# A ring tile of their own for the modulation units, and X's rows read back two per pair, in a one-core mLSTM, convolution and SwiGLU step

## The chip, the cores and the metric

The kernel runs on one core of a Trainium2 chip. The metric is the device time of one launch in microseconds; lower is better. The time before is the median of three runs: 1648.85 us, from 1646.58 to 1649.88.

## The reference

One layer of a diffusion backbone works on 640 tokens (128 of a context, 512 latent) of width 1024:

```python
mod = silu(cond) @ w_mod + b_mod                     # nine vectors of 1024 per condition
sh1, sc1, g1, shm, scm, gm, sh2, sc2, g2 = split(mod, 9)
h = rmsnorm(x, norm_g[0]) * (1 + sc1) + sh1
x = x + 0.5 * g1 * swiglu(h, ffn1_w1, ffn1_w2)       # (silu(a) * b) @ w2, inner width 2816
h = rmsnorm(x, norm_g[1]) * (1 + scm) + shm
z = h @ w_in + b_in                                  # q, k, v, o, gates, b, c, x, two merge gates
ml = (o * norm(mlstm_bidir(q, k, v, ...))) @ w_ml_out
sc = (bg * conv3(cg * xs)) @ w_sc_out
x = x + gm * ((sigmoid(gml) * ml + sigmoid(gsc) * sc) @ w_o)
h = rmsnorm(x, norm_g[2]) * (1 + sc2) + sh2
x = x + 0.5 * g2 * swiglu(h, ffn2_w1, ffn2_w2)       # then a final rmsnorm
```

All inputs are float32. There are two conditions (context and latent), so each of the nine modulation vectors is a product of two rows with a 1024 x 1024 piece of `w_mod`.

## The kernel before

The 640 tokens are two halves of 320. Activations lie transposed, 128 channels by 320 tokens. For float32 accuracy each operand is split into a high and a low part (ScalarE, ACT, copies the high part, line 75; VectorE, DVE, subtracts for the low one, line 79), and each product takes three matmuls on TensorE (PE; lines 288 to 290, in `three`).

**Elements.** The work is a list of elements. A plain element (`plain_el`) multiplies one block of a weight matrix, 128 columns by all rows, with both halves. A pair element (`pair_el`) does two blocks by two with seven products in place of eight; the sums of weights it needs are made by DVE (`ws`, line 270). The FFN runs in three groups of inner blocks (8, 8, 6), each with its w1 pairs and then its w2 blocks; the w2 blocks of the last group have 6 x 128 rows, 384 KB. PSUM tiles `ps` (four) take the products; DVE evacuates them, on line 360 in an FFN's w1 pairs, on 1020 and 2032 and 2072 in the products with w2, w_ml_out and w_sc_out.

**Weight loads.** `load_more` issues them on SyncE's queue (SP), in the order of one list `raws`, and each takes the next tile of a ring. A weight block and a modulation unit are both `[128, 1024]` float32 (512 KB) and share the ring `wr` with five tiles; a half tile `wq` serves the summed pairs. An instruction on SP waits until the ring's oldest tile has been read for the last time, and what is behind it in SP's queue waits as well. `cast_more` makes the casts up to four ahead of PE in the program, with six tiles each of `wh` and `wl`.

**Modulation units.** While other work runs, the vectors needed later are formed from `w_mod` in units of 512 KB. `mod_half` uses PE for them (line 649). `mod_dve` uses DVE: for each of two 128-row pieces and each condition a multiply and add with a column of silu(cond) (lines 767 and 769, accumulating into `ma`, `x` or `H` tiles). `with_own` and `with_units` hang units onto elements: the load goes behind the element's own loads in `raws`, and the reads are run as fillers among its products. In `with_units`, `places` says how many units each element gets; without it they are spread evenly.

**X.** The residual X (eight tiles, 128 x 640) is moved to DRAM while an FFN runs (`xd<-x`) and read back by `x_in` on GpSimd's queue (POOL) for the last group. `x_whole` reads all eight rows at one point of that group's third pair. The same function `more_of` serves both FFNs. Saved activation halves come back on the same queue (`HT3h`, `HT4h` and so on, line 1045).

Of the kernel before, what the change touches and what calls it, by code (L numbers as in the profile page):

```python
# [7 lines left out]
F32 = mybir.dt.float32  # L8
# [4 lines left out]
P = 128  # L13
D = 1024
KT = 8
# [29 lines left out]
def mixer_step(ctx: ExitStack, tc: tile.TileContext, x_prompt, x_sample, state_C, state_n, state_m,  # L45
# [33 lines left out]
            V.tensor_sub(lo, raw, f32(hi))  # L79


    RAWB, HALFB, OPB, SB, AHEAD = 5, 1, 6, 3, 4
    raws, ops = [], []
    rtile, optile, rdone = {}, {}, set()
    ptr = {"dma": 0, "sum": 0, "cast": 0, "use": 0, "held": 0, "hold": False, "cap": 1 << 20}
    fill = []
    turns, accs = {"wr": [], "wq": []}, []

    def drain(left=0):
        while len(fill) > left:  # L90
# [2 lines left out]
    def load_more(upto=1 << 20):  # L93
        while ptr["dma"] < min(upto, len(raws)):
            n = ptr["dma"]
            kind = getattr(raws[n], "kind", "wr")
            seq, bufs = turns[kind], RAWB if kind == "wr" else HALFB
            if len(seq) >= bufs and seq[-bufs] not in rdone:
                return
            seq.append(n)  # L100
            rtile[n] = ring.tile([P, 1024 if kind == "wr" else 512], F32, name=kind, bufs=bufs)
            raws[n](rtile[n])
            if hasattr(raws[n], "more"):
                accs.append((n, raws[n].more))
            ptr["dma"] += 1
# [89 lines left out]
    def element(raws_, ops_, emit):  # L195
        return {"raws": raws_, "ops": ops_, "emit": emit}
# [419 lines left out]
    PO = {}  # L616
# [92 lines left out]
    def with_own(pairs, ch, *last):  # L709

        us, fs = zip(*[mod_half(ch, half, True) for half in range(2)])
        out = []
        for p, el in enumerate(pairs):
            el = dict(el, raws=list(el["raws"]))
            fill = []
            if p < 4:
                units = us[p // 2][2 * (p % 2):2 * (p % 2) + 2]
                at_ = len(el["raws"])
                el["raws"] += [load for load, _ in units]

                def go(units=units, at_=at_, el=el):
                    tiles = [raw(el["base"] + at_ + i) for i in range(2)]
                    for i in range(2):
                        units[i][1](tiles[i])
                    rdone.update((el["base"] + at_, el["base"] + at_ + 1))
                    load_more()
                fill = [step(lambda: None), step(go), step(lambda: None)]
            if p == 2:
                fill[0] = step(fs[0][0])
                fill[2:] = [step(f) for f in fs[0][1:]]  # L730
            if p == 4:
                fill = [step(fs[1][0]), step(lambda: None)] + [step(f) for f in (*fs[1][1:], *last)]
            el["fill"] = fill
            out.append(el)
        return out

    def mod_mid(ch, half):
        us, fs = mod_half(ch, half)
        els = []
        for i, (load, emit) in enumerate(us):  # L740
            def go(w, emit=emit, last=(i == 3)):
                emit(w)
                if last:
                    soon.append(fs[0])
                    lazy.extend(fs[1:])
            els.append(dict(element([load], [], go), calm=True))
        return els

    def mod_dve(ch, halves, wide, joint=False):
# [54 lines left out]
    def with_units(main, units, spare=0, places=None):  # L804
# [3 lines left out]
        e = 0  # L808
        post = []
        due = [sum(places[:i + 1]) for i in range(len(main))] if places else None  # L810
        for i, el in enumerate(main):
# [4 lines left out]
            while e < m and (e < due[i] if places else e * n < (i + 1) * m):  # L816
                load, fns, more = units[e]
                at_ = len(el["raws"])
                el["raws"].append(load)
                for j, fn in enumerate(fns):  # L820
                    def go(fn=fn, at_=at_, el=el, last=(j == len(fns) - 1)):
                        fn(raw(el["base"] + at_))
# [383 lines left out]
    hd = {(o, k, i): hdr[8 * q + 2 * k + i] for q, o in enumerate(("T3", "T4")) for k in range(4) for i in range(2)}  # L1206
    PO["u_x"] = ExitStack()
    PO["un"] = 15

    def open_u():  # L1210
        PO["u"] = PO["u_x"].enter_context(pool("u"))
# [67 lines left out]
    def first_head(blocks):  # L1279
# [11 lines left out]
        def two(k0):  # L1291
# [1 line left out]
                for i, col0 in enumerate((0, DFF)):  # L1293
                    half_rows(ffn1_w1, col0, k0)(t[:, 512 * i:512 * i + 512])
            return load
        loads = [two(0), blocks[2][0]] + [u[0] for u in units[:RING]] + [two(4)] + [b[0] for b in blocks[3:]]
        part = lambda t, c: {"raws": [t], "n": 512, "src": lambda o: rtile[o["base"] + t][:, c:c + 512]}
        l2 = 2 + RING
        ops_ = [part(0, 0), part(0, 512), part(1, 0), part(1, 512), part(l2, 0), part(l2, 512)]
# [135 lines left out]
    def close_early():  # L1435
        early_x.close()
        st_x.close()
        PO["hq"] = ctx.enter_context(pool("hq", side="right"))

    uel = [step(lambda i=i: up[i][1](EARLY_T["up", i])) for i in range(4)]  # L1440
    qsc, qsh = [step(f) for f in UPQ[0][0]], [step(f) for f in UPQ[1][0]]
# [34 lines left out]
    prog += qsh[1:]  # L1476
    later = [lambda h=h, k=k: scale_x(h, k, RBS[h]) for h in (0, 1) for k in range(4, 8)]
    ptr["cap"] = 0
    def x_whole():
        for m in range(KT):  # L1480
            x_in(m)

    def x_end():
        while PO["x_end"]:
            PO["x_end"].pop(0)()

    def more_of(p):
        return {0: {p: {0: [lambda: h_away("T3", "T4")]}}, 1: {0: {4: [x_end]}},
                2: {0: {4: [x_end, lambda: PO.pop("xs")]}, 2: {1: [x_whole]}}}
    head, els = ffn(ffn1_w1, ffn1_w2, G1, after_lists(1, SHM), first_head, 3, (8, 8, 6), more_of(4),  # L1490
                    ({4, 5, 6, 7}, {4, 5, 6, 7}, ()), {0, 2}, {0: (2, 2, 1), 1: (2, 2, 1), 2: (3, 2)})
    PO["ma_x"] = ExitStack()
# [2 lines left out]
        gate_weights()  # L1495

    def open_ma():
        PO["ma"] = PO["ma_x"].enter_context(pool("ma"))

    def ma_wide():  # L1500
# [612 lines left out]
    conv = []  # L2113
    for m in range(0, KT, 2):
        if m:
            conv += [pair_el(*cx_pair(m), G), pair_el(*cx_pair(m + 1), G)]
        conv.append(pair_el(*bg_pair(m), G, spare_v=True))
    conv += weave([pair_el(*gsc_pair(m)) for m in range(0, KT, 2)], [step(lambda: None)] * 3 + [step(t_in(0))])
    prog += with_units(conv, mod_dve(SH2, (0,), m_wide), places=[1, 0, 0] * 3 + [1] + [0] * 4)
# [21 lines left out]
    def y_part(m, h):  # L2141
        def f():
# [4 lines left out]
            for i in range(3):  # L2147
                if h:
                    if m == 0:
                        YT[1, i] = ring.tile([P, 1024], F32, name="wr", bufs=RAWB)  # L2150
                    V.tensor_mul(YT[1, i][:, m * P:(m + 1) * P], p[:, i * P:(i + 1) * P],
                                 FN[q][:, (m % 2) * P:(m % 2 + 1) * P])
                    continue
# [95 lines left out]
```

## Time and profile before

| | |
|---|---|
| median of three runs | 1648.85 us |
| profiled execution | 1645.83 us, of which 1643.9 us is its span |
| PE, DVE, ACT, POOL busy | 99%, 80%, 54%, 20% of the span |
| DMA | 248.68 MB, mean 151 GB/s |
| clock granted to TensorE | 0.997 on average |
| largest wait of PE inside the program | 3.1 us, on DVE line 360 |

The profile comes from one execution. A group row ends with busy time and mean duration in ns; a row of waits gives the engine and line that waited, the engine and line that ended the wait, total, number and longest; a row of the timeline gives start, duration, engine, line, operation, `out<-in` and, in brackets, idle time of the engine just before and what ended it. Buffer numbers are left out of names there. In a row of windows the numbers after the window are the length and, for PE, PE's weight loads, DVE, ACT and POOL, the busy time; then the granted clock of TensorE (PEclk), DMA's share and GB/s.

### The profile page before, as it was taken

Reading aid. Unit: us, or ns where it says so; the run is one execution under the profiler, and the core shown is the slowest. Engines: PE = TensorE matmul, PEld = TensorE weight load, DVE = VectorE, ACT = ScalarE, POOL = GpSimd, SP = SyncE. Lnnn points to the kernel's source line nnn. Section 1 sums busy time; section 2 is a strip of 40 time slices with the busy share of each in tenths; the row PEclk is TensorE's granted clock in tenths of the full one; section 3 lists DMA queues with packets and bytes.
Section 4 is the critical chain, followed back from the end, with each engine's and each line's share of the span. In section 5 each row is a group of like instructions: output and inputs, shape, how many; then the busy total and the mean of one; then the engine's idle time right before and its main releaser. Section 6 shows DMA issues by size and latency. Waiting matters only on the chain.

```text
span 1643.9 us, 29669 instructions
## 1 busy us (share of the span) xinstructions
PE 1620.0 (99%) x10997; PEld 1573.2 (96%) x10997; DVE 1308.9 (80%) x2738; ACT 883.1 (54%) x1957; POOL 325.5 (20%) x457
## 2 busy tenths in 40 slices
PE   8999999999999999999999999999999999999998
PEld 5999999999989999999999999999999999999997
DVE  6878878978778878788897899879778877786765
ACT  5656555645466656555561455542276665565543
POOL 2132311130021322121121222001133113113002
PEclk9999999999999999999999999999999999999999
DMA  9698966793452434342367433457468768468522
GB/s 323 179 263 174 231 137 135 183 279 113 132 179 81 114 90 107 72 118 68 97 196 243 120 103 91 111 160 225 133 177 182 157 134 197 102 137 194 170 81 64
DMA packets 333200, 248.68 MB, mean 151 GB/s; under 512 B 11763, under 2 KB 306042, under 8 KB 333056
## 3 DMA queue, kind: packets, MB, share of 16 engines
q1 hardware_dynamic: 278256, 168.84, 35.8%
q0 software_dynamic: 54768, 77.95, 21.7%
q8 instruction: 86, 1.41, 0.4%
q14 instruction: 58, 0.48, 0.1%
q10 hardware_dynamic: 32, 0.01, 0.0%
HBM read 210.48 MB, written 36.28 MB: 150 GB/s over the span
## 4 chain that ended last, share of the span: by engine, by line
PE 84%; DVE 6%; DMA 3%; ACT 3%; issue 2%; SPq 1%; POOL 0%; ACTq 0%; DVEq 0%; POOLq 0%
PE ps L288 26%; PE ps L289 25%; PE ps L290 25%; DMA wr<-in_ffn_w_dram 3%; DVE wl L79 2%; PE ax L1793 2%; PE ax L1824 2%; PE ax L1796 1%; ACT wh L75 1%; PE ax L1770 1%; DVE ws L270 1%; ACT Uh L934 0%; SPq L627 0%; DVE Uh L926 0%; PE ax L778 0%
## 5 line engine op out<-in xcount | busy, mean ns | idle before, releaser
L79 DVE TENSOR_TENSOR wl<-wr,wh 128x512 fp32r<-128x512 f32 (+1 forms) x397 | 277.9, 709 | 86.2 <-ACT wh L75 84.1
L79 DVE TENSOR_TENSOR wl<-ws,wh 128x512 fp32r<-128x512 f32 x308 | 212.9, 691 | 62.9 <-ACT wh L75 62.5
L75 ACT CAST wh<-wr 128x512 fp32r<-128x512 f32 (+1 forms) x399 | 235.7, 606 | 36.8 <-DMA wr<-in_w_ml_out_dram 14.0
L75 ACT CAST wh<-ws 128x512 fp32r<-128x512 f32 x308 | 189.1, 620 | 97.9 <-DVE ws L270 83.2
L288 PE MATMUL ps<-HT4h,wh 128*128 128x320 f32 x440 | 139.5, 317 | 4.2 <-DVE t L360 4.0
L289 PE MATMUL ps<-HT4l,wh 128*128 128x320 f32 x440 | 137.1, 312 | 0.6 <-DVE HT4l L79 0.5
L288 PE MATMUL ps<-Uh,wh 128*128 128x320 f32 x440 | 137.3, 312 | 0.0
L290 PE MATMUL ps<-HT4h,wl 128*128 128x320 f32 x440 | 136.6, 310 | 0.0
L289 PE MATMUL ps<-Ul,wh 128*128 128x320 f32 x440 | 136.0, 309 | 0.0
L290 PE MATMUL ps<-Uh,wl 128*128 128x320 f32 x440 | 135.7, 308 | 0.0
L288 PE MATMUL ps<-HT3h,wh 128*128 128x320 f32 x388 | 122.0, 314 | 0.7 <-ACT ps L347 0.5
L288 PE MATMUL ps<-H11h,wh 128*128 128x320 f32 x376 | 119.6, 318 | 0.5 <-ACT H11h L75 0.5
L289 PE MATMUL ps<-HT3l,wh 128*128 128x320 f32 x388 | 119.9, 309 | 0.0
L290 PE MATMUL ps<-HT3h,wl 128*128 128x320 f32 x388 | 119.9, 309 | 0.0
L235 POOL DMA_DIRECT2D wr<-in_ffn_w_dram x48 | 62.3, 1448 | 282.6 <-DMA wr<-in_ffn_w_dram 115.9
L289 PE MATMUL ps<-H11l,wh 128*128 128x320 f32 x376 | 117.0, 311 | 0.7 <-DVE H11l L79 0.4
L288 PE MATMUL ps<-H21h,wh 128*128 128x320 f32 x376 | 117.5, 312 | 0.0
L290 PE MATMUL ps<-H11h,wl 128*128 128x320 f32 x376 | 116.6, 310 | 0.0
L290 PE MATMUL ps<-H21h,wl 128*128 128x320 f32 x376 | 116.3, 309 | 0.0
L289 PE MATMUL ps<-H21l,wh 128*128 128x320 f32 x376 | 116.0, 309 | 0.0
L288 PE MATMUL ps<-H22h,wh 128*128 128x320 f32 x344 | 107.9, 314 | 0.0
L289 PE MATMUL ps<-H22l,wh 128*128 128x320 f32 x344 | 106.5, 310 | 0.4
(489 smaller groups left out, 4943.7 us busy)
## 6 DMA issues: line engine op xcount, KB each, us to landing
wr<-in_ffn_w_dram SPq DMA_DIRECT2D x94, 512.0 KB, 5.7
wr<-in_w_in_dram SPq DMA_DIRECT2D x72, 512.0 KB, 3.9
wr<-in_w_mod_dram SPq DMA_DIRECT2D x59, 512.0 KB, 4.3
xd<-x POOLq DMA_DIRECT2D x56, 320.0 KB, 6.9
wr<-in_ffn_w_dram SPq DMA_DIRECT2D x52, 256.0 KB, 4.4
wr<-in_ffn_w_dram POOLq DMA_DIRECT2D x48, 256.0 KB, 5.4
x<-xd POOLq DMA_DIRECT2D x24, 320.0 KB, 8.0
early<-in_w_mod_dram SPq DMA_DIRECT2D x13, 512.0 KB, 8.9
```

The costliest lines, as they stand in the source:

```text
L75: A.copy(hi, raw)
L79: V.tensor_sub(lo, raw, f32(hi))
L235: queue.dma_start(t[:, 512 * o:512 * o + 512].rearrange("p (k n) -> p k n", k=4), dap(w, (row0 + 512 * half) * ncol + col0, [[ncol, P], [P ...
L270: engine.tensor_add(t, part(o, a), part(o, b))
L288: PE.matmul(ps, hi[:, ws], ah, start=start, stop=False, skip_group_check=True)
L289: PE.matmul(ps, hi[:, ws], al, start=False, stop=False, skip_group_check=True)
L290: PE.matmul(ps, lo[:, ws], ah, start=False, stop=stop, skip_group_check=True)
L1770: PE.matmul(p[:, :P], S["k", dt][:, sl], S["q", dt][:, sl], start=(dt == 0), stop=(dt == 1))
L1793: PE.matmul(p2[:, :DH + 1], S["q", dt][:, sl], S["C"][d][:, dt, :], start=(dt == 0), stop=(dt == 1))
L1796: PE.matmul(p1[:, :DH + 1], S["p", ch][:, d, :], PO["vt"][:, ch, :], start=True, stop=True)
L1824: PE.matmul(p[:, :DH + 1], kw[:, dt * P:(dt + 1) * P], PO["vt"][:, ch, :], start=True, stop=True)
```

## The change

There are two parts. First, units no longer share the five tiles of `wr`. `RAWB` gives `wr` four tiles, a new kind `wu` one, and a new kind `wv` one, which lives in a pool of its own from `close_early` to `open_ma` and serves the first FFN's first group alone. In `with_own` each two units take `wu` and `wv`. In `with_units` with `places` the first unit of an element takes `wu`, others `wr`; without, every other unit takes `wu`. `mod_mid` alternates, the third early unit of `first_head` takes `wu`, and so does one of three tiles of the last output. Second, `x_whole` is gone: the steps at index 1 and 4 of four pairs of the last group (2 to 5) each read one row of X. The line that builds `conv` is only written in another way.

```diff
@@ -79,12 +79,18 @@
             V.tensor_sub(lo, raw, f32(hi))
 
 
-    RAWB, HALFB, OPB, SB, AHEAD = 5, 1, 6, 3, 4
+    RAWB, OPB, SB, AHEAD = {"wr": 4, "wu": 1, "wv": 1, "wq": 1}, 6, 3, 4
     raws, ops = [], []
     rtile, optile, rdone = {}, {}, set()
     ptr = {"dma": 0, "sum": 0, "cast": 0, "use": 0, "held": 0, "hold": False, "cap": 1 << 20}
     fill = []
-    turns, accs = {"wr": [], "wq": []}, []
+    turns, accs = {k: [] for k in RAWB}, []
+
+    def of_kind(kind, load):
+        def f(t):
+            load(t)
+        f.kind = kind
+        return f
 
     def drain(left=0):
         while len(fill) > left:
@@ -94,11 +100,12 @@
         while ptr["dma"] < min(upto, len(raws)):
             n = ptr["dma"]
             kind = getattr(raws[n], "kind", "wr")
-            seq, bufs = turns[kind], RAWB if kind == "wr" else HALFB
+            seq, bufs = turns[kind], RAWB[kind]
             if len(seq) >= bufs and seq[-bufs] not in rdone:
                 return
             seq.append(n)
-            rtile[n] = ring.tile([P, 1024 if kind == "wr" else 512], F32, name=kind, bufs=bufs)
+            rtile[n] = (PO["wv"] if kind == "wv" else ring).tile([P, 512 if kind == "wq" else 1024], F32, name=kind,
+                                                                 bufs=bufs)
             raws[n](rtile[n])
             if hasattr(raws[n], "more"):
                 accs.append((n, raws[n].more))
@@ -716,7 +723,7 @@
             if p < 4:
                 units = us[p // 2][2 * (p % 2):2 * (p % 2) + 2]
                 at_ = len(el["raws"])
-                el["raws"] += [load for load, _ in units]
+                el["raws"] += [of_kind(kind, load) for kind, (load, _) in zip(("wu", "wv"), units)]
 
                 def go(units=units, at_=at_, el=el):
                     tiles = [raw(el["base"] + at_ + i) for i in range(2)]
@@ -743,7 +750,7 @@
                 if last:
                     soon.append(fs[0])
                     lazy.extend(fs[1:])
-            els.append(dict(element([load], [], go), calm=True))
+            els.append(dict(element([of_kind(("wu", "wr")[i % 2], load)], [], go), calm=True))
         return els
 
     def mod_dve(ch, halves, wide, joint=False):
@@ -816,7 +823,8 @@
             while e < m and (e < due[i] if places else e * n < (i + 1) * m):
                 load, fns, more = units[e]
                 at_ = len(el["raws"])
-                el["raws"].append(load)
+                other = any(getattr(q, "kind", "") == "wu" for q in el["raws"]) if places else e % 2
+                el["raws"].append(of_kind("wr" if other else "wu", load))
                 for j, fn in enumerate(fns):
                     def go(fn=fn, at_=at_, el=el, last=(j == len(fns) - 1)):
                         fn(raw(el["base"] + at_))
@@ -1206,6 +1214,7 @@
     hd = {(o, k, i): hdr[8 * q + 2 * k + i] for q, o in enumerate(("T3", "T4")) for k in range(4) for i in range(2)}
     PO["u_x"] = ExitStack()
     PO["un"] = 15
+    PO["wv_x"] = ExitStack()
 
     def open_u():
         PO["u"] = PO["u_x"].enter_context(pool("u"))
@@ -1293,7 +1302,7 @@
                 for i, col0 in enumerate((0, DFF)):
                     half_rows(ffn1_w1, col0, k0)(t[:, 512 * i:512 * i + 512])
             return load
-        loads = [two(0), blocks[2][0]] + [u[0] for u in units[:RING]] + [two(4)] + [b[0] for b in blocks[3:]]
+        loads = [two(0), blocks[2][0]] + [u[0] for u in units[:RING - 1]] + [of_kind("wu", units[RING - 1][0]), two(4)] + [b[0] for b in blocks[3:]]
         part = lambda t, c: {"raws": [t], "n": 512, "src": lambda o: rtile[o["base"] + t][:, c:c + 512]}
         l2 = 2 + RING
         ops_ = [part(0, 0), part(0, 512), part(1, 0), part(1, 512), part(l2, 0), part(l2, 512)]
@@ -1436,6 +1445,7 @@
         early_x.close()
         st_x.close()
         PO["hq"] = ctx.enter_context(pool("hq", side="right"))
+        PO["wv"] = PO["wv_x"].enter_context(pool("wv"))
 
     uel = [step(lambda i=i: up[i][1](EARLY_T["up", i])) for i in range(4)]
     qsc, qsh = [step(f) for f in UPQ[0][0]], [step(f) for f in UPQ[1][0]]
@@ -1476,17 +1486,14 @@
     prog += qsh[1:]
     later = [lambda h=h, k=k: scale_x(h, k, RBS[h]) for h in (0, 1) for k in range(4, 8)]
     ptr["cap"] = 0
-    def x_whole():
-        for m in range(KT):
-            x_in(m)
-
     def x_end():
         while PO["x_end"]:
             PO["x_end"].pop(0)()
 
     def more_of(p):
         return {0: {p: {0: [lambda: h_away("T3", "T4")]}}, 1: {0: {4: [x_end]}},
-                2: {0: {4: [x_end, lambda: PO.pop("xs")]}, 2: {1: [x_whole]}}}
+                2: {0: {4: [x_end, lambda: PO.pop("xs")]},
+                    **{2 + p: {i: [lambda m=2 * p + i // 3: x_in(m)] for i in (1, 4)} for p in range(4)}}}
     head, els = ffn(ffn1_w1, ffn1_w2, G1, after_lists(1, SHM), first_head, 3, (8, 8, 6), more_of(4),
                     ({4, 5, 6, 7}, {4, 5, 6, 7}, ()), {0, 2}, {0: (2, 2, 1), 1: (2, 2, 1), 2: (3, 2)})
     PO["ma_x"] = ExitStack()
@@ -1495,6 +1502,7 @@
         gate_weights()
 
     def open_ma():
+        PO["wv_x"].close()
         PO["ma"] = PO["ma_x"].enter_context(pool("ma"))
 
     def ma_wide():
@@ -2113,7 +2121,7 @@
     conv = []
     for m in range(0, KT, 2):
         if m:
-            conv += [pair_el(*cx_pair(m), G), pair_el(*cx_pair(m + 1), G)]
+            conv += [pair_el(*cx_pair(m + i), G) for i in range(2)]
         conv.append(pair_el(*bg_pair(m), G, spare_v=True))
     conv += weave([pair_el(*gsc_pair(m)) for m in range(0, KT, 2)], [step(lambda: None)] * 3 + [step(t_in(0))])
     prog += with_units(conv, mod_dve(SH2, (0,), m_wide), places=[1, 0, 0] * 3 + [1] + [0] * 4)
@@ -2147,7 +2155,8 @@
             for i in range(3):
                 if h:
                     if m == 0:
-                        YT[1, i] = ring.tile([P, 1024], F32, name="wr", bufs=RAWB)
+                        YT[1, i] = ring.tile([P, 1024], F32, name=("wu", "wr")[i > 0],
+                                             bufs=RAWB[("wu", "wr")[i > 0]])
                     V.tensor_mul(YT[1, i][:, m * P:(m + 1) * P], p[:, i * P:(i + 1) * P],
                                  FN[q][:, (m % 2) * P:(m % 2 + 1) * P])
                     continue
```

The order of the instructions on PE, SP and POOL is the same in both kernels; what differs on SP is the tile that a load takes and so what it waits for. Line numbers move by 7 to 9. Of SP's queue in the first FFN's last group, these are the rows around the w2 blocks before (`wr_5273`, `wr_5408` and `wr_5466` are units, the others blocks):

```order
L620 DMA wr_5273<-in_w_mod_dram 128x2x512
L218 DMA wr_5333<-in_ffn1_w2_dram 128x6x128
L620 DMA wr_5408<-in_w_mod_dram 128x2x512
L218 DMA wr_5428<-in_ffn1_w2_dram 128x6x128
L620 DMA wr_5466<-in_w_mod_dram 128x2x512
L218 DMA wr_5578<-in_ffn1_w2_dram 128x6x128
L218 DMA wr_5580<-in_ffn1_w2_dram 128x6x128
```

and now:

```order
L627 DMA wu_5329<-in_w_mod_dram 128x2x512
L225 DMA wr_5331<-in_ffn1_w2_dram 128x6x128
L627 DMA wu_5568<-in_w_mod_dram 128x2x512
L225 DMA wr_5570<-in_ffn1_w2_dram 128x6x128
L627 DMA wu_5628<-in_w_mod_dram 128x2x512
L225 DMA wr_5630<-in_ffn1_w2_dram 128x6x128
L225 DMA wr_5632<-in_ffn1_w2_dram 128x6x128
```

The units `wu_5329`, `wu_5568` and `wu_5628` follow each other in one tile, so each load waits for the last read of the unit before it; blocks `wr_5570` and `wr_5630`, formerly `wr_5428` and `wr_5578`, stand behind them as before.

On DVE at the same place (line 79 the low casts, 769 the reads of a unit, 1020 the evacuations), before:

```order
L79 TENSOR_TENSOR Ul_5535<-t3_5499,Uh_5534 128x320
L79 TENSOR_TENSOR wl_5541<-wr_5428,wh_5540 128x512
L79 TENSOR_TENSOR wl_5545<-wr_5428,wh_5544 128x256
L794 TENSOR_TENSOR modT_131<-ax_5525,bmT_129 128x4 x2
L769 SCALAR_TENSOR_TENSOR ma_5267<-wr_5273,cm_93,ma_5267 128x512 x2
L769 SCALAR_TENSOR_TENSOR ma_5310<-wr_5273,cm_93,ma_5310 128x512 x2
L1020 SCALAR_TENSOR_TENSOR x_4936<-ps_5538,modT_131,x_4936 128x128
L1020 SCALAR_TENSOR_TENSOR x_4936<-ps_5538,modT_131,x_4936 128x192
L1020 SCALAR_TENSOR_TENSOR x_4936<-ps_5539,modT_131,x_4936 128x320
L79 TENSOR_TENSOR wl_5603<-wr_5578,wh_5602 128x512
L79 TENSOR_TENSOR wl_5607<-wr_5578,wh_5606 128x256
L769 SCALAR_TENSOR_TENSOR ma_5267<-wr_5408,cm_93,ma_5267 128x512 x2
```

and now:

```order
L79 TENSOR_TENSOR Ul_5533<-t3_5497,Uh_5532 128x320
L801 TENSOR_TENSOR modT_131<-ax_5523,bmT_129 128x4 x2
L776 SCALAR_TENSOR_TENSOR ma_5263<-wu_5329,cm_93,ma_5263 128x512 x2
L776 SCALAR_TENSOR_TENSOR ma_5306<-wu_5329,cm_93,ma_5306 128x512 x2
L1028 SCALAR_TENSOR_TENSOR x_4938<-ps_5536,modT_131,x_4938 128x128
L1028 SCALAR_TENSOR_TENSOR x_4938<-ps_5536,modT_131,x_4938 128x192
L1028 SCALAR_TENSOR_TENSOR x_4938<-ps_5537,modT_131,x_4938 128x320
L79 TENSOR_TENSOR wl_5593<-wr_5570,wh_5592 128x512
L79 TENSOR_TENSOR wl_5597<-wr_5570,wh_5596 128x256
L776 SCALAR_TENSOR_TENSOR ma_5263<-wu_5568,cm_93,ma_5263 128x512 x2
L776 SCALAR_TENSOR_TENSOR ma_5306<-wu_5568,cm_93,ma_5306 128x512 x2
```

The two casts of the block behind unit 5408 (now 5568) have moved from ahead of the reads of unit 5273 (now 5329) to behind the evacuation after them, and those of the next block behind the reads of the next unit and its evacuation.

SP's queue in w_sc_out before, where units and blocks alternate in one ring:

```order
L620 DMA wr_13743<-in_w_mod_dram 128x2x512
L218 DMA wr_13771<-in_w_sc_out_dram 128x8x128
L620 DMA wr_13773<-in_w_mod_dram 128x2x512
L218 DMA wr_13857<-in_w_sc_out_dram 128x8x128
L620 DMA wr_13859<-in_w_mod_dram 128x2x512
L218 DMA wr_13945<-in_w_sc_out_dram 128x8x128
L620 DMA wr_13947<-in_w_mod_dram 128x2x512
L218 DMA wr_14031<-in_w_sc_out_dram 128x8x128
```

and now, where every other unit is `wu`:

```order
L627 DMA wr_13739<-in_w_mod_dram 128x2x512
L225 DMA wr_13767<-in_w_sc_out_dram 128x8x128
L627 DMA wu_13859<-in_w_mod_dram 128x2x512
L225 DMA wr_13861<-in_w_sc_out_dram 128x8x128
L627 DMA wr_13863<-in_w_mod_dram 128x2x512
L225 DMA wr_13949<-in_w_sc_out_dram 128x8x128
L627 DMA wu_14033<-in_w_mod_dram 128x2x512
L225 DMA wr_14035<-in_w_sc_out_dram 128x8x128
```

The blocks `wr_13767` to `wr_14035` stand where `wr_13771` to `wr_14031` did; `wr_13861` (formerly `wr_13857`) and `wr_14035` (formerly `wr_14031`) are now behind a unit that takes the tile of the unit two before it, and wait until that one has been read. On DVE and ACT the only other move is here, two casts that come after a unit's reads and an evacuation and not before them.

POOL's queue at the reads of X in the first FFN now, with what each waits for (DMASW counts earlier DMAs of this queue):

```order
L1041 DMA xd_133<-x_852 128x640 [waits DMASW2_49,DVE_49,Activation_49]
L1041 DMA xd_133<-x_853 128x640 [waits DMASW3_49,Activation_49]
L2093 DMA x_4938<-xd_133 128x640 [waits DMASW4_49]
L2093 DMA x_5006<-xd_133 128x640 [waits DMASW5_49]
L2093 DMA x_5097<-xd_133 128x640 [waits DMASW6_49]
L2093 DMA x_5165<-xd_133 128x640 [waits DMASW7_49]
L2093 DMA x_5265<-xd_133 128x640 [waits DMASW0_49]
L2093 DMA x_5333<-xd_133 128x640 [waits DMASW1_49]
L2093 DMA x_5422<-xd_133 128x640 [waits DMASW2_49]
L2093 DMA x_5478<-xd_133 128x640 [waits DMASW3_49]
```

Before, the same eight stand in the same place with the same waits; only the tiles' numbers, which count allocations, have spread out.

## The prediction

> **What bounds the kernel now.** I read the page first (busy times, then the chain), then the waits by engine, then the timeline and windows around every load that the change moves.
>
> ```profile
> PE 1620.0 (99%) x10997; PEld 1573.2 (96%) x10997; DVE 1308.9 (80%) x2738; ACT 883.1 (54%) x1957; POOL 325.5 (20%) x457
> PE ps L288 <- DVE t L360: 4.0, 3, 3.1
> PE ps L288 <- ACT ps L332: 0.6, 1, 0.6
> PE ps L288 <- ACT H11h L75: 0.5, 1, 0.5
> SPq L218 <- DVE ws L270: 527.0, 63, 20.2
> ```
>
> TensorE (PE) is busy for 99% of the span, so a change gains only what PE still waits for, and loses whatever makes PE wait. The largest wait inside the program is one of 3.1 us, behind line 360 on VectorE (DVE). SyncE's queue (SPq) does wait, 527 us in one group alone: it stands at the head of a ring that is full, which is how loads are issued many microseconds before their casts. This lead is what the change spends.
>
> The 3.1 us wait stands where X's rows come back in the first FFN:
>
> ```profile
> x<-xd POOLq DMA_DIRECT2D x8, 320.0 KB, 8.9
> wr<-in_ffn_w_dram SPq DMA_DIRECT2D x3, 512.0 KB, 12.3
> 344.77 0.37 SPq L620 DMA_DIRECT2D wr<-in_w_mod_dram  x1
> 350.31 5.12 SPq L218 DMA_DIRECT2D wr<-in_ffn_w_dram  x2
> 354.38 0.67 DVE ma L769
> 355.07 12.31 DMA wr<-in_ffn_w_dram
> 367.40 0.69 DVE L270 TENSOR_TENSOR ws<-wr 128x512 f32<-128x512 f32 x1 [4.15 <-DMA wr<-in_ffn_w_dram]
> 371.02 0.64 PE L288 MATMUL ps<-HT4h,wh 128*128 128x320 f32 x1 [3.11 <-DVE t L360]
> 370.00:372.00 2.00, 0.98 (x4) 0.98 (x5) 2.00 (x4) 0.62 (x1) 0.00 (x0) 0.50 0.00 0
> 372.00:376.80 4.80, 4.80 (x20) 4.80 (x20) 3.92 (x9) 2.31 (x5) 0.00 (x0) 0.50 0.39 113
> 376.80:380.00 3.20, 3.20 (x23) 3.20 (x23) 2.83 (x6) 1.76 (x4) 0.00 (x0) 1.00 0.55 164
> ```
>
> The first two rows are transfers issued from 342 to 370 us (number, size, median us to landing); then come two rows of SyncE's queue, a unit and two weight blocks, and two pieces of the chain. The weight load issued at 355.07, right after a unit's last read by DVE, shares the chip with eight transfers of X and takes 12.3 us. DVE stands still for 4.15 us, PE for 3.11. The windows (PEclk is the third number from the end) show the granted clock at 0.50 from PE's restart to 376.80: 5.8 us at half speed, 2.9 us lost. The whole place costs about 6.0 us, and it is the only sizeable prize.
>
> **The change part by part.** *X two rows per pair.* POOL's queue has the eight `x<-xd` in the same order, directly behind each other, in both kernels (rows in the section on the change), and nothing is put between them. In the program they wait for no engine, only for earlier DMAs, so writing them later in the program does not hold them back: they go out together as before. Cost and gain 0, in the second FFN too, whose PE has no such wait.
>
> *A ring of one for units.* A unit's load must now wait for the last read (L769) of the unit before it, and since SyncE issues in order, each weight block queued behind that unit waits too. I took every SP load's new releasers and put them on the times of this trace. Where the lead stays 7 us or more I count nothing: all of the mLSTM, the convolution and the second FFN. The early units (to about 165 us, ring tiles `wu` and `wv`) come earlier, up to 21 us; with PE's waits there being single ones of at most 0.6 us (rows above), that is worth −0.3 us, between −1.1 and 0. Four places are left.
>
> *(1) 344 to 372 us.* The unit issued at 344.8 goes out at 355.1 (behind the `DVE ma L769` above), and the two weight blocks at 355.6 and 356.0 instead of 350.3 and 355.1: all three inside X's burst. Against this, the burst ends earlier, since 0.5 MB of SP's loads are no longer mixed into its first half. If all is short the place is gone: −6.0. If the last block lands 4 us later: +4. The nearest row is the 12.3 us landing; with 0.9 us later issue I take +0.8.
>
> *(2) 416 to 450 us, the w2 blocks of the last group.*
>
> ```profile
> 415.99 0.37 SPq L620 DMA_DIRECT2D wr<-in_w_mod_dram  x1
> 418.76 0.37 SPq L218 DMA_DIRECT2D wr<-in_ffn_w_dram  x1
> 426.39 12.69 SPq L218 DMA_DIRECT2D wr<-in_ffn_w_dram  x5
> 429.69 2.98 DVE L769 SCALAR_TENSOR_TENSOR ma<-wr,cm,ma 128x512 f32<-128x512 f32 x4
> L75 ACT CAST wh<-wr 128x512 fp32r<-128x512 f32 (+1 forms) x399 | 235.7, 606 | 36.8 <-DMA wr<-in_w_ml_out_dram 14.0
> 434.76 1.02 DVE L79 TENSOR_TENSOR wl<-wr,wh 128x512 fp32r<-128x512 f32 x2 [1.05 <-ACT wh L75]
> wr<-in_ffn_w_dram SPq DMA_DIRECT2D x6, 384.0 KB, 3.4
> 436.44 0.31 PE L288 MATMUL ps<-Uh,wh 128*128 128x320 f32 x1
> 441.72 0.31 PE L288 MATMUL ps<-Uh,wh 128*128 128x320 f32 x1
> ```
>
> The first row is unit `wr_5408`, the second block `wr_5428`, the third begins with block `wr_5578`; the two PE rows are the first products with these blocks. Now unit 5408 waits for the read that starts at 429.69 and ends at 432.67. It may end up to 1.0 us sooner, since the cast pair ahead of it on DVE has moved behind; I put the block at 432.1 instead of 418.76. Alone it lands in 3.4 us; behind the unit's 512 KB, whose own landing is of the same order, I take 4.6 (up to 6.2, the longest group median below). 436.7, plus 0.6 for ACT's cast (606 ns in its group) and 0.7 for DVE's (the 1.02 row is the pair), gives 438.0, where PE wants the low half at 436.7: 1.3 us idle. Then DVE finishes that block's second cast (438.4), reads unit 5408 (2.98, to 441.4), and only then does the next unit go out, with block 5578 behind it at 441.8: landed 446.4, cast 447.7, wanted 442.0. So PE is 5.7 us behind in all (3.3 with 3.4 us landings, 8.9 with 6.2), and the second gap is 4.4 us. That is longer than the 3.11 us gap after which the clock was halved, so I add its price of 2.9: +8.6, between 3.3 and 11.8.
>
> The Trainium skill, "TensorE: Matmul & The Clock Gate", Part 1, says that half rate comes after an idle window of about 3.4 us and ends after about as long a busy one; the trace fits roughly, with 3.11 us idle and 5.8 us at 0.50. By that rule the loss would be half of 3.4, 1.7 us, and the sum 1.2 us less.
>
> *(3) 847 to 895 us, w_ml_out.*
>
> ```profile
> wr<-in_w_ml_out_dram SPq DMA_DIRECT2D x5, 512.0 KB, 6.2
> 851.02 0.37 SPq L620 DMA_DIRECT2D wr<-in_w_mod_dram  x1
> 856.09 0.37 SPq L218 DMA_DIRECT2D wr<-in_w_ml_out_dram  x1
> 862.43 0.75 DVE L769 SCALAR_TENSOR_TENSOR x<-wr,cm,x 128x512 f32<-128x512 f32 x1
> 863.89 1.28 DVE L79 TENSOR_TENSOR wl<-wr,wh 128x512 fp32r<-128x512 f32 x2
> 875.10 0.93 DVE L2032 SCALAR_TENSOR_TENSOR x<-x,ps 128x320 f32<-128x320 f32 x2 [2.01 <-PE ps L290]
> 847.00:904.00 57.00, 56.61 (x388) 55.60 (x387) 43.67 (x76) 19.77 (x39) 12.53 (x22) 1.00 0.83 268
> ```
>
> The unit of 851.02 now waits for the L769 that ends at 863.2; the block of 856.09 goes out at 863.7 and lands near 869.5, where DVE wanted to cast it at 863.89. DVE blocks 6 us; PE does not need the cast before it has ended the block whose evacuation starts at 875.10 by PE's release, but the evacuations (L2032) stand behind it on DVE. PE can run two blocks ahead of them (four `ps` tiles, two to a block), some 5 us of cover. Every second block repeats this, with a smaller delay, as the unit reads slip along. DVE has 13 us free in these 57. I take +3, between 0 (all covered) and 7.
>
> *(4) 1086 to 1155 us, w_sc_out and the first w_o blocks.*
>
> ```profile
> wr<-in_w_sc_out_dram SPq DMA_DIRECT2D x3, 512.0 KB, 4.4
> 1098.15 0.37 SPq L218 DMA_DIRECT2D wr<-in_w_sc_out_dram  x1
> 1141.93 0.37 SPq L218 DMA_DIRECT2D wr<-in_w_o_dram  x1
> 1103.38 0.31 PE L288 MATMUL ps<-Bh,wh 128*128 128x320 f32 x1
> 1105.01 0.47 DVE L769 SCALAR_TENSOR_TENSOR HT2h<-wr,cm,HT2h 128x256 f32<-128x256 f32 x1
> 1105.40 0.48 DVE L2072 TENSOR_TENSOR x<-ps,x 128x320 f32<-128x320 f32 x1
> 1108.39 1.29 DVE L79 TENSOR_TENSOR wl<-wr,wh 128x512 fp32r<-128x512 f32 x2
> 1109.00:1150.00 41.00, 41.00 (x287) 39.78 (x286) 39.84 (x95) 10.88 (x23) 7.04 (x14) 1.00 0.74 223
> ```
>
> The block of 1098.15 now stands behind a unit that waits for the L769 ending at 1105.48: issued 1106.0, landed 1110.4, cast by ACT 1111.1, against 1108.39 where DVE wants it. DVE blocks 2.7 us. That happens for every second block, four times, from the block of 1098.15 to that of 1141.93 (one in about 14.6 us): 10.8 us. DVE is busy 39.84 of 41 us here, so it makes up 1 us at most, and the evacuation L2072, which at 1105.40 runs 2.0 us behind PE's turn to the next block (1103.38), leaves some 4 us of PSUM cover once, not four times. 10.8 − 4 = +7 (rounded), between 0 and 10.8.
>
> Sum: −0.3 + 0.8 + 8.6 + 3 + 7 = +19.1 us. The profiled execution took 1645.83 us (span 1643.9 and 1.93 around it), 3.0 under the median of the runs: 1645.83 + 19.1 + 3.0 = 1668.
>
> **The rivals.** *It gains.* The three loads at place 1 land in time because the burst is no longer slowed by the first of them; the 6.0 us go, and the later blocks are covered by the casts, which at place 3 run some 10 us ahead of PE (863.89 against 875). For it: place 1 is the largest PE wait of the trace. Against it: the loads are issued later, into the same burst, and must land by about 364 for DVE not to wait; the turning point is place 2 costing less than 6. It would give 1648.85 − 6.0 = 1643.
>
> *No change.* Place 1 stays as it is and every delayed block lands before PE needs it. For it: casts lead PE widely. Against it: at place 2 the block is issued 4.3 us before its product, less than landing and cast. It gives 1649.
>
> *Only place 2 bites.* DVE's blocking at 3 and 4 disappears in PSUM cover: +8.6 with the half clock, +5.7 without, so 1655 to 1657. For it: DVE's 13 us free at place 3, one stall of 2.7 less than 4 at place 4. Against it: the stalls at place 4 follow each other while DVE is 97% busy.
>
> *It is worse.* All terms at their upper ends, 4 + 11.8 + 7 + 10.8 = 33.6 us, with gaps long enough for the half clock at a second place: 1682.
>
> A rule speaks for the losing side as well: the Trainium skill, "DMA: Bandwidth & Descriptors", section "Rules for kernel authors", advises to issue a DMA early and wait on it late. The 527 us of SPq's waits show that the kernel before does so; the price is in the sum already.
>
> **How the numbers follow.** Likeliest is the sum: 0.43, at 1668 (its own range 1660 to 1675). Only place 2: 0.25. Worse: 0.12. It gains: 0.11. No change: 0.09. Runs of this kernel differ by about 0.2% (3.3 us), and less than that cannot be told from no change. Faster is 0.11, same 0.09, slower 0.80. The range from 1649 to 1678 leaves out the gain, half of no change and half of the worst case, 2 in 10.
>
> **What would show it.** Right: SP rows of the w2 units near 432 and 439 to 442, each directly behind an L769; a PE gap above 3 us near 442 to 448 with PEclk 0.50 after it; DVE waiting for `DMA wr` in w_sc_out before every second cast pair, 2 to 3 us each; eight `x<-xd` issued within 8 us, as before. Wrong: x reads spread out over the last group, no gap at 371, or wl casts in w_sc_out without a DMA wait ahead of them. The forecast fails if a load queued behind a unit lands in 3.4 us or less, or if the PSUM cover is wider than I count.

## The result, and the profile after

The changed kernel takes 1688.24 us (median of four runs, 1683.82 to 1689.89) against 1647.71 us for the kernel before in the same comparison: ratio 1.0241, interval 1.0217 to 1.0265. It is some 40 us slower; the forecast was slower, at 1668 us, with a range that ends at 1678. The profiled execution took 1688.68 us, 42.9 us more than that of before.

The head of the page after, and PE's longest waits in it:

```profile
PE 1635.9 (97%) x10997; PEld 1583.9 (94%) x10997; DVE 1308.1 (78%) x2738; ACT 883.5 (52%) x1957; POOL 325.6 (19%) x457
PE ps L295 <- ACT wh L75: 6.6, 3, 4.3
PE ps L295 <- ACT t L364: 6.6, 1, 6.6
PE ps L295 <- DVE t L367: 6.4, 4, 3.6
PE ps L295 <- DVE x L2040: 4.4, 1, 4.4
PE ps L295 <- DVE x L2080: 4.0, 1, 4.0
```

PE's busy time rises by 15.9 us although it runs the same 10997 matmuls. Some 10 us of that are time at half clock: inside the program PE works for 25.4 us in stretches at half clock now and for 5.8 us before, and half of such time is lost. The rest is PE's work drawn out around short stops, most of it (4.1 us) in w_sc_out. The waits, one of 3.1 us before, are now five long ones (3.6 to 6.6 us). In PE's timeline these are five of the rows below; two shorter ones, of 1.21 and 1.87 us, are shown with them because they come up again:

```profile
122.18 0.63 PE L295 MATMUL ps<-HT4h,wh 128*128 128x320 f32 x1 [6.57 <-ACT t L364]
379.04 0.63 PE L295 MATMUL ps<-HT4h,wh 128*128 128x320 f32 x1 [3.61 <-DVE t L367]
444.70 0.41 PE L295 MATMUL ps<-Uh,wh 128*128 128x320 f32 x1 [1.21 <-ACT wh L75]
454.94 0.63 PE L295 MATMUL ps<-Uh,wh 128*128 128x320 f32 x1 [4.27 <-ACT wh L75]
936.41 0.61 PE L295 MATMUL ps<-HT1h,wh 128*128 128x320 f32 x1 [4.41 <-DVE x L2040]
1163.86 0.61 PE L295 MATMUL ps<-Bh,wh 128*128 128x320 f32 x1 [3.95 <-DVE x L2080]
1576.48 0.41 PE L295 MATMUL ps<-HT4h,wh 128*128 128x320 f32 x1 [1.87 <-DVE t L367]
```

PE's order is the same in both kernels, so the start of the same matmul in the two traces gives a ledger: how much later PE is behind each place than ahead of it, with the half clock that follows.

| place (time before) | delay added in the profile | predicted |
|---|---|---|
| first group of the first FFN (116 to 125 us) | +7.4 | −0.3 |
| last group's w1, X's burst (371) | −0.6 | +0.8 |
| last group's w2 (436 to 445) | +9.1 | +8.6 |
| w_ml_out (889 to 916) | +9.7 | +3 |
| w_sc_out, w_o (1117 to 1162) | +13.5 | +7 |
| second FFN (1535) | +3.7 | 0 |
| sum | 42.8 | 19.1 |

The w2 place went as written, to half a microsecond. SP's queue there, DVE's casts and the clock after the gap:

```profile
438.54 0.37 SPq L627 DMA_DIRECT2D wu<-in_w_mod_dram  x1
439.00 0.42 SPq L225 DMA_DIRECT2D wr<-in_ffn_w_dram  x1
448.63 0.37 SPq L627 DMA_DIRECT2D wu<-in_w_mod_dram  x1
454.92 1.03 DVE L79 TENSOR_TENSOR wl<-wr,wh 128x512 fp32r<-128x512 f32 x2 [4.18 <-ACT wh L75]
453.80:461.00 7.20, 6.06 (x23) 5.83 (x24) 5.68 (x11) 2.02 (x5) 0.00 (x0) 0.53 0.75 186
```

The unit goes out only at 438.54 (before: 415.99), the block behind it at 439.00, and the second pair at 448.63 after the reads of the first unit; the window shows PEclk 0.53 for 7.2 us.

### The profile page after: what moved, and what is told of

It is laid out like the page before. It is cut to its first block, busy times and chain, and to the rows that moved or that the text cites. A ratio compares the mean times of both kernels' runs of the same rounds, so it can differ in the third digit from the quotient of the medians.

```text
span 1686.8 us, 29653 instructions
## 1 busy us (share of the span) xinstructions
PE 1635.9 (97%) x10997; PEld 1583.9 (94%) x10997; DVE 1308.1 (78%) x2738; ACT 883.5 (52%) x1957; POOL 325.6 (19%) x457
## 3 DMA queue, kind: packets, MB, share of 16 engines
q8 instruction: 86, 1.41, 0.3%
## 4 chain that ended last, share of the span: by engine, by line
PE 74%; DVE 11%; DMA 8%; ACT 4%; issue 2%; SPq 1%; POOL 0%; ACTq 0%; DVEq 0%
PE ps L295 23%; PE ps L296 22%; PE ps L297 22%; DMA wr<-in_ffn_w_dram 4%; DVE wl L79 3%; PE ax L1801 2%; PE ax L1832 2%; ACT wh L75 1%; DMA wr<-in_w_sc_out_dram 1%; DMA wr<-in_w_ml_out_dram 1%; PE ax L1804 1%; DVE x L776 1%; DVE HT2h L776 1%; DMA wr<-in_w_o_dram 1%; DVE ws L277 1%
```

## The experiments

The kernels take one part of the change each. "Alone" means: X's rows as in the change, all loads in the five tiles as before, and only one stretch of the program with the change's kinds.

**What X does, and a first attempt that measured something else** (`x_only`). Outside the stretch under test a load took the four `wr` tiles and `wu` in strict turn:

```diff
+            if kind != "wq" and zones[n] not in OWN:
+                kind = "wu" if ptr["turn"] % 5 == 4 else "wr"
```

> X's rows are read back two per pair as in the change, but the loads take the five tiles as before: four wr and one wu in strict turn, units and blocks alike. Theory (the reads are issued in POOL's queue as before, nothing holds them): the time of before, 1648 +- 2 us, eight reads within 8 us, the 3.1 us gap of PE near 371 still there. Rival (the reads do spread): 1642 and no gap near 371, or a delay of the second FFN that is owed to X.

Measured: 1659.11 us, ratio 1.0069 (1.0049 to 1.0090). Neither: X cannot be blamed before it is separated from the strict turn, which is not what the ring of five does. That ring takes the tile that was released first in the program, and units and blocks are not released in the order in which they were loaded. In `x_alone` the choice is the tile that was released first, which makes every load of SP wait for what it waits for before; these are two lines of the edit:

```diff
+                at = min(range(5), key=lambda i: (-1 if slots[i] is None else rdone.when.get(slots[i], 1 << 30), i))
+                kind = "wu" if at == 4 else "wr"
```

> X's rows are read back two per pair as in the change; every load takes, of the five tiles, the one that was released first in the program, as the single ring of before does (the run x_only took them in strict turn instead). Theory (the reads of X are not held by anything, and the 11.7 us of x_only are the price of the strict turn): the time of before, 1647.5 +- 2 us, PE's gap near 371 still 3 us. Rival (the 11.7 us came from X's part): 1659.

Measured: 1645.67 us against 1645.66, ratio 1.0000 (0.9985 to 1.0015). In its trace every load of SP goes out within 1.3 us of its moment before, reckoned from PE's progress, and the eight reads of X within 7 us (354.8 to 361.7). X's part of the change does nothing, and the split of one pool of five into four and one costs 11.7 us when its tiles are used in turn (1659.11 against 1647.44).

Three runs had been made on the strict turn:

> As x_only, but the first FFN's first group (with_own) loads its units into wu and wv as in the change; all else takes five tiles in turn. Theory (two units and the next pair's blocks are released at one moment and share the DMA engines with POOL's adding loads): PE waits 5 to 7 us near 120, in all +7 to +8 us, 1655 to 1656. Rival (the gap near 120 comes with the rings of the rest of the program, for example with the third unit of the head): no gap, 1648.

> As x_only, but only the eight w_ml_out elements use the change's kinds (every other unit wu, the rest wr in four tiles). Theory (every second block stands behind a unit that waits for the reads of the unit two before it; the cost is made in this place): DVE waits about 6 us three times, PE +8 to +11 us, 1656 to 1659. Rival (the cost comes from lateness that was built up before 850 us): +0 to +3, 1648 to 1651.

> As x_only, but only w_sc_out and the first five w_o elements use the change's kinds. Theory (as in only_ml, with four waits of DVE of about 4 us and no free time on DVE): +12 to +15 us, 1660 to 1663, with a half-clock stretch after one PE gap near 4 us. Rival (the landing is longer only because of earlier lateness): +5 to +7, as the prediction priced it.

Measured: 1654.48, 1664.92 and 1668.59 us (1.0043, 1.0112, 1.0128). They mix a place with the price of the turn elsewhere (the first is even faster than `x_only`) and do not give the price of a place. The following are on the ring of `x_alone`.

**The places one by one.**

> As x_alone, but the units and blocks of the first FFN after its first w1 pairs (165 to 450 us) take the change's kinds. Theory: PE gaps of about 1.2 and 4.3 us at the last group's w2 blocks and 3.4 us at half clock after them, +8 to +9 us, 1656. Rival (the second gap only comes because the early 7 us of delay shifted loads against each other): below +4.

Measured: 1658.79 us, 1.0075 (1.0045 to 1.0104). The gaps at the w2 blocks are 1.22 and 3.92 us, as in the whole change, and in the profile this place costs 8.0 us; the theory holds, the rival (below +4) falls. The profiled execution, the slowest of the four (1663.65 us), also lost 6.7 us in the first group, where this kernel is the one before, so the median is not the price of the tested stretch alone.

> As x_alone, but only the eight w_ml_out elements take the change's kinds. Theory (each second block is issued behind a unit that waits for the reads of the unit two before it): DVE stands 6 us three times, PE +8 to +11 us, 1656 to 1659. Rival (strict turn in the rest made the 5.8 us between x_only and only_ml; alone it is covered by PSUM): +0 to +4.

Measured: 1656.61 us, 1.0060 (1.0042 to 1.0078), as the theory has it; in the profile the place costs 8.0 us. DVE's low casts in w_ml_out show the waits:

```profile
872.54 1.29 DVE L79 TENSOR_TENSOR wl<-wr,wh 128x512 fp32r<-128x512 f32 x2 [5.87 <-ACT wh L75]
888.14 1.29 DVE L79 TENSOR_TENSOR wl<-wr,wh 128x512 fp32r<-128x512 f32 x2 [5.71 <-ACT wh L75]
903.95 1.30 DVE L79 TENSOR_TENSOR wl<-wr,wh 128x512 fp32r<-128x512 f32 x2 [6.43 <-ACT wh L75]
```

Every second cast pair waits about 6 us, and the third wait is no shorter than the first.

> As x_alone, but only w_sc_out and the first five w_o elements take the change's kinds. Theory: four waits of DVE of about 4 us, +12 to +15 us, 1660 to 1663. Rival (as the prediction priced it, waits of 2.7 us): +5 to +8.

Measured: 1659.87 us, 1.0079 (1.0050 to 1.0107). In the profile the place costs 11.5 us, a little under the theory and above the rival; as in `ffn1_alone` the profiled execution (1663.71 us) lost another 5.9 us in the first group, which is not part of the test. The waits in its trace are these:

```profile
1108.67 1.29 DVE L79 TENSOR_TENSOR wl<-wr,wh 128x512 fp32r<-128x512 f32 x2 [2.28 <-ACT wh L75]
1119.49 1.29 DVE L79 TENSOR_TENSOR wl<-wr,wh 128x512 fp32r<-128x512 f32 x2 [3.48 <-ACT wh L75]
1137.88 1.29 DVE L79 TENSOR_TENSOR wl<-wr,wh 128x512 fp32r<-128x512 f32 x2 [4.23 <-ACT wh L75]
1156.10 1.29 DVE L79 TENSOR_TENSOR wl<-wr,wh 128x512 fp32r<-128x512 f32 x2 [3.37 <-ACT wh L75]
```

> As x_alone, but only the first FFN's first group (with_own) loads its units into wu and wv as the change does. PE's gap near 120 was 0.4 us in the profile of before, 2.8 in that of x_alone, 5.0 and 4.6 in two kernels that are the same as before up to there, so it varies by itself. Theory (both units and the next pair's blocks go out at one moment and share the DMA engines with POOL's adding loads): the gap is 5 to 7 us in every run, +5 to +7 us, 1651 to 1653. Rival (the gap after is the luck of one run): +0 to +2, within the spread of before.

Measured: 1654.48 us, 1.0041 (1.0026 to 1.0056). The gap is 6.92 us here, 7.12 in `only_own`, 6.90 in `pool_units` below and 6.57 in the change: it is there in every profile of a kernel with these kinds.

> As x_alone, but only the second FFN has the change's rings: no units are loaded there, so its weight blocks have four tiles and the fifth (wu) stands empty. Theory (a block is loaded one place later in the ring, into the burst of X's reads): a PE gap of about 2 us near 1535 with half clock behind it, +3 us, 1649. Rival (the gap near 1576 after the change came from the delays before it): +0.

Measured: 1648.73 us, 1.0014 (0.9998 to 1.0029), and no gap of 1 us or more in its second FFN. The interval takes in both. `pool_units` below has the same ring of four in its second FFN and no stop there in its profile either, so the ring alone did not make one in these two executions; what the 3.7 us of the second FFN belong to stays open.

The five ratios alone add up to +2.7%, the whole change is +2.4%. A likely part of the difference is the stall of the first group, which comes by itself in some executions and so enters medians of four runs; the prices of single places are better read from the profiles.

**Is it the one tile, or the queue?** `pool_units` is the changed kernel with one edit, the queue from which the units of w_ml_out, w_sc_out and w_o are loaded:

```diff
-    prog += with_units(ml, mod_dve(GM, (1,), m_wide) + mod_dve(SH2, (1,), m_wide))
+    prog += with_units(ml, mod_dve(GM, (1,), m_wide, G) + mod_dve(SH2, (1,), m_wide, G))
```

(the same for `sc + wo`; the last argument is the queue of the loads).

> The changed kernel, but the units of w_ml_out, w_sc_out and w_o are loaded by POOL's queue, so no weight block stands behind a unit in SP's. Tiles and kinds are those of the change. Theory (the wait of the queue is what costs, not the one tile): the 8 to 14 us of each of the two places go down to 0 to 3, 1688 - 20 = 1668, and SP's blocks go out as their casts free tiles. Rival (one unit tile is too few, DVE waits for the unit itself): DVE waits for wu, 1685 or more.

Measured: 1663.97 us, ratio 1.0098 (1.0071 to 1.0124) to before, where the change has 1.0241. Both places are gone from its ledger: PE is 17.9 us late at 455 us and 18.1 us late at 1600 us (times of the kernel before). The w2 place, whose units stay on SP's queue, keeps its cost (+9.2), and the stop in the second FFN does not come in this execution; the time is 4 us below the 1668 that was expected. Its DVE casts in w_sc_out, and a window of that stretch:

```profile
1133.05 1.29 DVE L79 TENSOR_TENSOR wl<-wr,wh 128x512 fp32r<-128x512 f32 x2
1147.24 1.29 DVE L79 TENSOR_TENSOR wl<-wr,wh 128x512 fp32r<-128x512 f32 x2
1100.00:1180.00 80.00, 80.00 (x555) 78.77 (x554) 72.90 (x170) 24.01 (x49) 18.07 (x30) 1.00 0.67 209
```

No wait is left ahead of the casts and PE is busy for all 80 us, with the same single tile for units. So one tile is enough; what cost some 24 us was that weight blocks stood behind a waiting unit in one queue.

**The first group.** In the change the two units of a pair go out together, and the block behind them 5 us sooner than before (first three rows after, then two before; line 225 is line 218 of before):

```profile
111.48 0.37 SPq L627 DMA_DIRECT2D wu<-in_w_mod_dram  x1
111.95 0.41 SPq L627 DMA_DIRECT2D wv<-in_w_mod_dram  x1
114.87 1.98 SPq L225 DMA_DIRECT2D wr<-in_ffn_w_dram  x1
111.19 2.05 SPq L620 DMA_DIRECT2D wr<-in_w_mod_dram  x2
120.17 0.37 SPq L218 DMA_DIRECT2D wr<-in_ffn_w_dram  x1
```

`own_half` keeps this order and halves the units' bytes; it leaves out half of the rows that the first group's modulation vector needs (one line of the edit):

```diff
+            nc.sync.dma_start(t[:, :512], dap(w_mod, 2 * kq * P * 9 * D + ch * D + half * 512, [[9 * D, P], [1, 512]]))
```

> As own_alone, but each of the eight units of the first group loads only its first 128 rows (256 KB in place of 512), and both products of a unit read them; the modulation vector that they make is left wrong. What is released and issued when stays as in own_alone. Theory (the loads that go out together crowd POOL's adding loads): the adding loads near 111 land in 8 us or less in place of 10 to 11, PE's gap near 120 falls from 6.9 to 0 to 3 us, +0 to +3 us, 1647 to 1650. Rival (it is the moment of issue, 3 us later for the first unit and the adds that follow it, not the bytes): the gap stays 5 us or more, 1652 to 1654.

Measured: 1644.62 us, 0.9982 (0.9971 to 0.9992), and no gap near 120. POOL's adding loads (two of 256 KB issued from 105 to 120 us: before, after, `own_alone`, `own_half`):

```profile
wr<-in_ffn_w_dram POOLq DMA_DIRECT2D x2, 256.0 KB, 7.5
wr<-in_ffn_w_dram POOLq DMA_DIRECT2D x2, 256.0 KB, 10.2
wr<-in_ffn_w_dram POOLq DMA_DIRECT2D x2, 256.0 KB, 10.6
wr<-in_ffn_w_dram POOLq DMA_DIRECT2D x2, 256.0 KB, 6.2
```

They land 3 us later with the change and sooner than before with half the bytes. So the stall hangs on the bytes that are released together: halving them alone removes it. The moment of issue is not separated from this: the earlier units of the group were halved too, and POOL's two adding loads go out at 109.03 and 111.18 us in `own_half`, at 111.01 and 113.62 in `own_alone`; how much of the stall is the later issue and how much the slower landing is not shown. The place is near its edge in any case: in three kernels whose first 165 us are those of before (`x_alone`, `ffn1_alone`, `sc_alone`) it showed 2.8 to 5.0 us in the one execution that was profiled, in others 1 us or less.

**A version that beats both** (`x_sync`). The kernel before, with the diff's spread steps and one more argument: the reads of X in the last groups go into SP's queue (`q` is `nc.sync` there and POOL's queue elsewhere; the line that passes it is left out here).

```diff
-        G.dma_start(X[m], xd[m])
+        q.dma_start(X[m], xd[m])
```

> The kernel before, with X's rows read back two per pair as in the change, but issued on SP's queue, where they stand between the weight loads and so do wait. Theory (the burst is what makes PE wait near 371): the eight reads spread over 40 us or more, PE's gap near 371 goes, with the half clock behind it, -4 to -7 us, 1640 to 1643. Rival (the restores of HT, not X, crowd the weight load): gap stays, 1646; or the weight loads behind the reads of X are late elsewhere: +2 or more.

Measured: 1641.60 us, ratio 0.9971 (0.9955 to 0.9988), about 5 us faster than before. The reads in the trace of this kernel, and two windows across the place:

```profile
L2082 SPq DMA_DIRECT2D x<-xd x8: 408/456/522, 372.6 to 416.8; - x8
360.00:372.00 12.00, 12.00 (x84) 12.00 (x83) 10.59 (x20) 6.42 (x14) 0.00 (x0) 1.00 0.42 130
372.00:380.00 8.00, 8.00 (x57) 8.00 (x55) 8.00 (x15) 4.20 (x8) 0.00 (x0) 1.00 0.58 177
```

Eight reads from 372.6 to 416.8 us in place of 351.8 to 359; PE is busy throughout and the clock stays at 1.00. The stall at 371 was X's burst, and the spread is worth what the prediction put on that place (6.0 us; 5.7 in the profile), once something holds the reads. SP's queue without the spread was not run.

## Why the prediction was wrong in size

Right: X's part does nothing (`x_alone`); the mechanism, blocks behind a unit that waits for the reads of the unit before (`pool_units` for places 3 and 4, SP's rows for place 2); place 2 to half a microsecond, half clock included; place 1, which barely moved in the profile. At place 2 some luck helped: the 2.9 us for the half clock came from one execution of another gap, and such a price changes with the moment at which the gap falls (last section). In `ffn1_alone` the gap of 3.92 us at the same place was followed by 3.4 us at half clock, in the change the one of 4.27 us by 6.8 us.

The steps that failed are four terms of the sum: one with the wrong sign, two too small, and one put at nothing.

- *The early units.* They "come earlier, up to 21 us", and that was put at "−0.3 us, between −1.1 and 0". Only the gain was bounded. Loads that go out sooner compete with those that were already the late ones, here POOL's adding loads: +7.4 in the profile of the change, +0.41% (6.8 us) in `own_alone`.
- *w_ml_out.* "Every second block repeats this, with a smaller delay": the waits are 5.9, 5.7 and 6.4 us. The block is issued when the unit's reads end, and these reads come after the wait for the block before, so the loop sets its own period and nothing slips back into place. The 13 us of free DVE time in 57 did not take this up, presumably since it lies elsewhere in the loop. +3 was +9.7 in the profile, +0.60% alone, with half clock after the 4.41 us gap, which the term left out.
- *w_sc_out.* The stalls were put at 2.7 us, with a landing of 4.4 us. That median came from loads that go out one at a time. In the change a unit, a block, a unit and a block go out within two microseconds, and the blocks land behind the 512 KB of a unit or more:

```profile
wu<-in_w_mod_dram SPq DMA_DIRECT2D x5, 512.0 KB, 4.2
wr<-in_w_sc_out_dram SPq DMA_DIRECT2D x6, 512.0 KB, 7.0
1151.26 0.37 SPq L627 DMA_DIRECT2D wu<-in_w_mod_dram  x1
1151.72 0.42 SPq L225 DMA_DIRECT2D wr<-in_w_sc_out_dram  x1
1152.19 0.57 SPq L627 DMA_DIRECT2D wr<-in_w_mod_dram  x1
1152.86 0.42 SPq L225 DMA_DIRECT2D wr<-in_w_sc_out_dram  x1
1170.71 0.37 SPq L627 DMA_DIRECT2D wu<-in_w_mod_dram  x1
1158.85 1.29 DVE L79 TENSOR_TENSOR wl<-wr,wh 128x512 fp32r<-128x512 f32 x2 [4.75 <-ACT wh L75]
```

  Between 1152.86 and 1170.71 the queue issues nothing. At place 2 the prediction had allowed for the unit ahead of the block and was right; at place 4 it had not. +7 was +13.5, with half clock behind the 3.95 us gap, which the term left out.
- *The second FFN.* Counted at nothing since the lead was 7 us or more, although its ring shrinks from five tiles to four. +3.7 in the profile of the change, +0.14% alone with an interval that takes in zero, nothing in the profile of `pool_units`: open.

Of the rivals, "worse" was the nearest (1682, chance 0.12); its upper ends were too low at places 3 and 4 (7 and 10.8), and it had no loss for the early units.

The Trainium skill, "DMA: Bandwidth & Descriptors", section "Issuing engines are not separate DMA queues", says that issuing from several engines only saves issue time, since all run on the same DMA engines. The bytes in these traces do share them (POOL's adding loads land 3 us later beside SP's units); but `pool_units` won some 24 us by another queue alone, because a load that waits holds those behind it. For a queue with waits in it the measurement decides.

## What to carry to other kernels

Before a load gets a tile of its own, ask what stands behind it in its queue: a ring of one turns the last read of its tile into a wait of everything that is issued after. Price such a loop as a loop (end of the reads, issue, landing behind whatever goes out with it, cast, reads), not as one stall that fades; and where loads come sooner, look for the slow transfer that they will meet. A step that is moved in the program moves in time only if something holds it there.

## What the runs showed of the hardware that was not expected

The half clock does not need a long gap, and a longer gap can go without it. The first three rows are the 1.87 us gap before 1576.48 in the changed kernel, the last three the 2.20 us gap before 378.19 in `own_alone`:

```profile
1573.46:1576.88 3.42, 1.55 (x10) 1.28 (x10) 3.35 (x6) 1.24 (x2) 0.00 (x0) 1.00 0.45 109
1576.88:1580.29 3.41, 3.41 (x15) 3.41 (x14) 2.53 (x6) 2.32 (x5) 0.00 (x0) 0.50 0.00 0
1580.29:1583.70 3.41, 3.41 (x25) 3.41 (x25) 2.82 (x6) 1.05 (x3) 0.00 (x0) 1.00 0.40 117
373.37:376.78 3.41, 2.62 (x18) 2.35 (x17) 2.20 (x4) 0.63 (x1) 0.00 (x0) 1.00 0.97 285
376.78:380.19 3.41, 2.00 (x13) 2.00 (x14) 3.02 (x6) 0.97 (x2) 0.00 (x0) 1.00 0.03 10
380.19:383.60 3.41, 3.41 (x26) 3.41 (x25) 2.92 (x6) 2.47 (x7) 0.00 (x0) 1.00 0.51 151
```

The windows are cut where the clock can change: in each of the 15 traces all its changes fall on one grid with steps of 3.41 us. The gap of 1.87 us lies within one step, the one of 2.20 us is split by the grid into 0.79 and 1.41. In all the traces together, the first 15 and the last 8 us left out, a step at full clock in which PE was idle for 1.87 us or more was followed by one at half clock, 31 times of 31; with 1.67 us or less it never was, and of three steps from 1.71 to 1.79 one was. A step at half clock with 0.54 us or less of idle time was followed by full clock, one with 0.62 us or more by another step at half clock. So a gap costs, beyond itself, nothing, or half of PE's time in one or two steps (up to 1.7 us each; once it was three), and which of these it is also depends on where the gap falls on the grid: the gap of 1.21 us at 444.70 was followed by no slow step, the one of 4.27 us by two.

The Trainium skill, "TensorE: Matmul & The Clock Gate", Part 1, speaks of an idle window of about 3.4 us that runs freely. The length and the fixed grid agree with the traces. That the window has to be idle throughout does not: here a step idle for a little over half was enough, and the measurement decides.
